# The first two feature tiles of a macaron FFN computed together, k tile by k tile, on one Trainium2 core

## The chip, the core and the metric

The kernel runs on one core of a Trainium2 chip. The metric is the device time of one execution in microseconds (us); the median of the runs of the kernel before is 1067.11 us (three runs, 1066.84 to 1070.1). Engines are named as in the profile: PE is the matrix engine (PEld its weight loads), ACT the scalar engine, DVE the vector engine, POOL the general one, SP the engine that only issues transfers. The names with a q (SPq, ACTq) are the queues on which an engine issues DMAs.

## The reference, cut to what matters

One decoder layer over 512 tokens, model width 1024, FFN width 2816. The change touches only how its first step begins:

```python
def rms_norm(x, g):
    xf = x.astype(jnp.float32)
    y = xf * lax.rsqrt(jnp.mean(xf * xf, axis=-1, keepdims=True) + EPS)
    return (y * g.astype(jnp.float32)).astype(x.dtype)

def swiglu_ffn(x, g, w_gate, w_up, w_down):
    h = rms_norm(x, g)
    return (jax.nn.silu(h @ w_gate) * (h @ w_up)) @ w_down

x = x + 0.5 * swiglu_ffn(x, ffn1_norm, ffn1_w_gate, ffn1_w_up, ffn1_w_down)
...
x = x + merged @ w_out
x = x + 0.5 * swiglu_ffn(x, ffn2_norm, ffn2_w_gate, ffn2_w_up, ffn2_w_down)
```

Between the two FFNs stand two attention branches, which the change leaves as they are.

## The kernel before, in words

**Layout.** x is kept transposed: 8 tiles `x[d]` of 128 model dimensions by 512 tokens. A product of one feature tile (128 of the 2816 features) runs over these 8 tiles, called k tiles here. Everything is float32 in accuracy: each operand is split into a high part that the matrix engine takes directly (`wh`, `xh`) and a rest (`wl`, `xl`), and each product is three matmuls, high by high, high by rest, rest by high. The high part of a weight is a copy on ACT, its rest a subtraction on DVE (`load_w`, L128 to L144, and `split_w`, L115 to L126). For some weights the rest is made otherwise: ACT writes the negated high part and POOL issues a DMA that adds the raw weight (the `adding` branch, L121 to L123). `prep` (L153) makes `xh` on ACT (L161) and `xl` on DVE (L162) from `x[d]` and the norm weight `gains`. The factor of the norm that depends on the token isn't applied to x but to the products.

**The norm's factor.** `square` (L164) squares `x[d]` on ACT, `add_square` (L170) adds the squares on DVE into one tile `ssq`, in a chain, one d after another. `norm_stats` (L177) is a generator with two steps. Its first step is eight tiny matmuls on `ssq` (L181), a small DVE operation (`v`, L183) and a power on POOL (`rstd`, L185). Its second step is four transposes on PE (L189) and a copy on DVE to `rb` (L191). `activate` (L299) needs `rb`: it multiplies gate and up by it, applies silu on ACT, and splits the result into `ah` and `al`.

**The begin block** (L765 to L800) has a hand written order for SP, ACT and DVE: what the code emits first, each of these engines does first. It loads x[0] on ACT's queue and all else on SP's: parts of the first feature tile's gate and up weights, the norm weights `gains`, the x tiles, and then the whole gate and up of the second feature tile (`raws`, L791). In between it emits the splits, `prep`s and `square`s in an order set by d. After the loop come the split of the second tile's gate with the fourth `add_square` inside it, the last four squares, the last four `add_square`s, and the split of the second tile's up. The buffers of `wh` and `wl` are three each and are used in turn, so a split waits until PE has finished with the weights that were made three splits earlier.

**The first FFN** (`ffn`, L202). PE's order is written out by hand throughout. First come the gate and up of feature tile 0 (L696 to L701): for each k tile three matmuls into bank `pg`, three into bank `pu`. Then the list `steps` runs: gate of tile 1 (`run_gate(1)`), up of tile 1, gate and up of tiles 2 and 3, eight steps with `w_down` for these four tiles (`run_down`), and then the steps of the remaining tiles, which take pairs of tiles with fewer products (`pair_steps`). Within gate 1, after k tile 3, PE does the first step of `norm_stats`, after k tile 6 the second (`at_k`, L354). `activate(0)` comes after gate 1, `activate(1)` after up 1. The rests of the weights of tiles 2 and 3 are made by ACT and a POOL DMA (`adding` where f > 1), that of tile 1 by DVE.

**Combinations.** `pair_steps` need x in other combinations (`combine`, L325), made for four k tiles with ten DVE operations and four ACT copies each. They need `rb`; from the first step on, two pieces of the twelve are emitted behind each step. They must stand ready when the first `pair_steps` product starts.

Of the kernel before, what the change touches and what calls it, by code (L numbers as in the profile page):

```python
# [12 lines left out]
F32 = mybir.dt.float32  # L13
F32R = mybir.dt.float32r
# [5 lines left out]
P = 128  # L20
T = 512
NT = T // P
D = 1024
KD = D // P
# [22 lines left out]
PLAIN = 4  # L47
# [8 lines left out]
def tile_hybrid_layer(ctx: ExitStack, tc: tile.TileContext, a: dict):  # L56
    nc = tc.nc
    V, S, G, PE = nc.vector, nc.scalar, nc.gpsimd, nc.tensor

    ctx.enter_context(tc.manual_schedule(engines={mybir.EngineType.PE}))  # L60
    const = ctx.enter_context(tc.tile_pool(name="const", bufs=1))
# [6 lines left out]
    def acc_tile(name):  # L68
        return psum.tile([P, T], F32, tag="acc", bufs=3, name=name)
# [21 lines left out]
    nhalf = const.tile([P, 8], F32, name="nhalf")  # L91
    G.memset(nhalf, -0.5)

    gains = const.tile([P, 3, KD], F32, name="gains")
    xa = const.tile([P, KD, T], F32, name="xa")
    x = [xa[:, d] for d in range(KD)]
    hg = const.tile([P, 4], F32, name="hg")
    bf = const.tile([P, H], F32, name="bf")
# [65 lines left out]
    def square(d, pool=None):  # L164
        sq = (tmp.tile([P, T], F32, tag="ssq", bufs=1, name="ssq") if d == 0 else
              pool.tile([P, T], F32, name=f"sq{d}") if pool else tmp_tile("sq"))
        S.activation(sq, x[d], AF.Square)
        return sq
# [33 lines left out]
    def ffn(n, nxt):  # L202
        wg, wu, wp, wd, wh_ = (a[f"w_{nm}{n}"] for nm in ("gate", "up", "pair", "down", "halves"))
        gi = 0 if n == 1 else 2
        with tc.tile_pool(name=f"ffn{n}", bufs=1) as ap, tc.tile_pool(name=f"halves{n}", bufs=1) as hp:
            act = {}

# [143 lines left out]

            held, pair0, rbs = [], [], []
            stats = norm_stats()
            at_k = (3, 6) if n == 1 else (1, 5)  # L354
            mid = {at_k[0]: lambda: next(stats), at_k[1]: lambda: held.append(next(stats))}

            class Step:

# [8 lines left out]
            def plain(src, f, run, adding=False, ahead=2):  # L367
                raw = {}

                def split():  # L370
                    return [t[:, :f * P].rearrange("p (n m) -> p n m", n=f)
                            for t in split_w(raw["a"][0], f * P, adding)]
                return Step(raw, [("a", f, src)], split, run, "a", ahead)
# [3 lines left out]
            def run_gate(f):  # L377
                def run(w):
                    pg[0] = fm_product(w, "pg", mid if f == 1 else {})
                    if f == 1:  # L380
                        activate(0, *pair0, held[0])
                        rbs.append(held[0])
                return run

            def run_up(f):
                def run(w):

                    pu = fm_product(w, "pu", {}, psum.tile([P, T], F32, tag="s", bufs=2, name="pu1") if f == 1 else None)
                    if f == 0:
                        pair0.extend((pg[0], pu))  # L390
                    else:
                        activate(f, pg[0], pu, rbs[0])
                return run
# [285 lines left out]
            gu_at = cycle(range(4))  # L679
            for lo, hi in GROUPS:  # L680
                for f in range(lo, min(hi, PLAIN)):
                    if f or not first:
                        steps += [plain(wg[f], KD, run_gate(f), f > 1), plain(wu[f], KD, run_up(f), f > 1)]
                for q in range(max(lo, PLAIN) // 2, hi // 2):
                    if ordered[0] is None:
                        ordered[0] = len(steps)
                    steps += pair_steps(q, 2 * q + 2 == hi, lo in HALVED)
                if lo in HALVED:
                    for s in range(2):
                        steps += halved_steps(lo, s)  # L690
                    continue
                ordered[1] = len(steps)
                steps += [plain(wd[d][:, lo:hi], hi - lo, run_down(d, lo, hi), ahead=1 if d == 1 else 2) for d in range(KD)]

            if first:
                pg[0], pu = acc_tile("pg"), acc_tile("pu")  # L696
                for k in range(KD):
                    for ps, w in zip((pg[0], pu), first):
                        PE.matmul(ps, w[k][0], xh[k], start=k == 0, stop=False)
                        PE.matmul(ps, w[k][1], xh[k], start=False, stop=False)  # L700
                        PE.matmul(ps, w[k][0], xl[k], start=False, stop=k == KD - 1)  # L701
                first.clear()
                pair0.extend((pg[0], pu))

            queue = [(i, ld) for i, st in enumerate(steps) for ld in st.loads]
            ws, used = {}, []
# [55 lines left out]
                later.popleft()[0]()  # L762


    first = [[], []]  # L765
    with tc.tile_pool(name="begin", bufs=1) as bp, tc.manual_schedule(
            engines={mybir.EngineType.SP, mybir.EngineType.Activation, mybir.EngineType.DVE}):
        squares = []
        S.dma_start(x[0], a["x"][:, 0, :])
        for d in range(KD):  # L770
            for dst, src, at in zip(first, ("w_gate1", "w_up1"), ({0: (0, 2), 2: (2, 8)}, {1: (0, 4), 4: (4, 8)})):
                if d in at:
                    lo, hi = at[d]
                    w = load_w(a[src][0][:, lo:hi], hi - lo, P, bp.tile([P, 1024], F32, name=f"raw{d}"))
                    dst += [(w[0][:, k], w[1][:, k]) for k in range(hi - lo)]
            if d:
                nc.sync.dma_start(x[d], a["x"][:, d, :])
            else:
                nc.sync.dma_start(gains, a["gains"])
            if d == 6:  # L780
                add_square(0, squares[0])
            if d > 5:
                add_square(d - 5, squares[d - 5])
            prep(d, 0)
            if d > 3:
                squares.append(square(d - 4, bp))
        raws = []
        for nm in ("w_gate1", "w_up1"):
            tag = next(raw_tags)
            raws.append((raw_tile(tag), tag))  # L790
            nc.sync.dma_start(raws[-1][0].rearrange("p (n m) -> p n m", n=KD), a[nm][1])  # L791

        def split_raw(raw, tag, between=None):
            ready.append(([t.rearrange("p (n m) -> p n m", n=KD) for t in split_w(raw, between=between)], tag))

        split_raw(*raws[0], lambda: add_square(3, squares[3]))
        squares += [square(d, bp) for d in range(4, KD)]
        for d in range(4, KD):
            add_square(d, squares[d])
        split_raw(*raws[1])  # L800
# [603 lines left out]
def _fm(w):  # L1404

    k, n = w.shape
    return w.reshape(k // P, P, n // P, P).transpose(2, 1, 0, 3)
# [22 lines left out]
def _layout(x, ffn1_norm, ffn1_w_gate, ffn1_w_up, ffn1_w_down, mix_norm, w_in, b_forget,  # L1430
            fox_q_norm, fox_k_norm, dsa_q_norm, dsa_k_norm, rel_bias,
            w_branch_a, w_branch_b, w_out, ffn2_norm, ffn2_w_gate, ffn2_w_up, ffn2_w_down):
    o = {}
    o["x"] = x.reshape(T, KD, P).transpose(2, 1, 0)
    o["gains"] = np.stack([g.reshape(KD, P).T for g in (ffn1_norm, mix_norm, ffn2_norm)], axis=1)
    o["hgain"] = np.stack([np.concatenate([g, g]) for g in (fox_q_norm, dsa_q_norm, fox_k_norm, dsa_k_norm)], axis=1)
    o["bforget"] = np.broadcast_to(b_forget, (P, H))
    for n, (g, u, dn) in ((1, (ffn1_w_gate, ffn1_w_up, ffn1_w_down)), (2, (ffn2_w_gate, ffn2_w_up, ffn2_w_down))):
        o[f"w_gate{n}"] = _fm(g)[:PLAIN]
        o[f"w_up{n}"] = _fm(u)[:PLAIN]  # L1440

        gu = np.stack([_fm(w)[PLAIN:].reshape(-1, 2, P, 2, HK, P) for w in (g, u)])
        o[f"w_pair{n}"] = gu.transpose(1, 2, 4, 3, 0, 5, 6).reshape(-1, 4, P, 2 * HK * P)
        o[f"w_down{n}"] = _fm(dn)

        dh = _fm(dn)[:, :, PLAIN:].reshape(2, 2, 2, P, -1, GK, 2, P)
        o[f"w_halves{n}"] = dh.transpose(4, 1, 0, 6, 3, 2, 5, 7).reshape(-1, 2, 4, P, 2 * GK, P)
    c = lambda lo, hi: w_in[:, lo:hi]
    o["w_s"] = _tm(np.concatenate([c(2056, 2120), c(2696, 2760), c(2120, 2184), c(1536, 1544), c(2760, 2768)], axis=1))[:, FIRST]
    o["w_fq"] = _tm256(c(0, 512))  # L1450
    o["w_fk"] = _tm256(c(512, 1024))
    o["w_fv"] = _tm256(c(1024, 1536))
    o["w_dq"] = _tm256(c(1544, 2056))
    o["w_iq"] = _fm(c(2184, 2696))
    o["w_ga"] = _fm(c(2768, 3792))
    o["w_gb"] = _fm(c(3792, 4816))
    o["w_ba"] = _fm(w_branch_a)
    o["w_bb"] = _fm(w_branch_b)
    o["w_out"] = _fm(w_out)
    dist = np.maximum(384 + np.arange(P)[:, None] - np.arange(T)[None, :], 0)  # L1460
    o["rel"] = rel_bias[_bucket(dist)].transpose(2, 0, 1)
    return {k: np.ascontiguousarray(v) for k, v in o.items()}
# [19 lines left out]
```

## Time and profile before

| | |
|---|---|
| median of three runs | 1067.11 us |
| the profiled execution, its own time | 1066.31 us |
| its span (first to last instruction) | 1064.6 us |
| granted clock of PE | 1.0 |

The profile is one execution on the chip. Its page gives each engine's busy time and share of the span. The timeline has a row per instruction or run of like instructions: start, duration, engine, line, operation, the tile written and, behind the arrow, the tiles read, shapes, count, and in brackets how long the engine sat idle before it and what released it. The view of waits sums such idle time by the two parties. The DMA view lists each kind of transfer with its size and the median time from issue to landing. The view of windows gives busy time per engine in stretches of the span, and at the end of each row the DMA engines' share and what they moved in GB/s.

### The profile page before, as it was taken

The numbers are of one execution on the slowest core, as the hardware profiler recorded it, in microseconds if no ns is written. First come the engines' busy times: TensorE is split into PE (matmuls) and PEld (weight loads), VectorE is DVE, ScalarE is ACT, GpSimd is POOL, SyncE is SP. The second block draws the span as 40 slices with busy tenths as digits, with TensorE's granted clock in tenths as the row PEclk, the third lists the DMA queues.
The fourth block names the chain that finished last, engine by engine and source line by source line (L and its number), as shares of the span: only waits on it lengthen the run. The fifth ranks groups of instructions, "written<-read, shape, count | busy, mean of one in ns | idle before, by whom it ended". The sixth has DMA issues, their size and how long they took to land.

```text
span 1064.6 us, 19527 instructions
## 1 busy us (share of the span) xinstructions
PE 1051.7 (99%) x7438; PEld 979.8 (92%) x7438; DVE 849.4 (80%) x1400; ACT 672.0 (63%) x1120; POOL 257.2 (24%) x325
## 2 busy tenths in 40 slices
PE   9999999999999999999999999999999999999998
PEld 7889999999999899999877788888889999999998
DVE  6987888887889689977777765853987888887887
ACT  6736765765687675576877665433736765775673
POOL 1100210120121024267777653000100210121111
PEclk9999999999999999999999999999999999999999
DMA  7743754666557358623323321532543665667554
GB/s 241 156 148 111 156 152 139 140 156 181 125 126 179 99 133 201 193 90 110 80 61 120 118 70 50 163 124 81 128 158 100 151 159 147 136 156 183 126 125 129
DMA packets 57917, 143.71 MB, mean 135 GB/s; under 512 B 6616, under 2 KB 15960, under 8 KB 57824
## 3 DMA queue, kind: packets, MB, share of 16 engines
q1 hardware_dynamic: 39888, 110.22, 34.0%
q0 software_dynamic: 17792, 31.99, 17.2%
q8 instruction: 58, 0.95, 0.4%
q10 hardware_dynamic: 144, 0.26, 0.1%
q14 instruction: 35, 0.29, 0.1%
HBM read 104.94 MB, written 3.42 MB: 102 GB/s over the span
## 4 chain that ended last, share of the span: by engine, by line
PE 47%; DVE 3%; POOL 2%; ACT 2%; issue 2%; POOLq 0%; DVEq 0%
PE pB L149 2%; PE pB L151 2%; PE pB L150 2%; PE pA L149 2%; PE pA L151 2%; PE pA L150 2%; PE ps_f L149 2%; PE ps_f L151 2%; PE ps_f L150 2%; PE ps_out L151 1%; PE ps_out L150 1%; PE ps_out L149 1%; PE dB L150 1%; PE dB L149 1%; PE dB L151 1%
## 5 line engine op out<-in xcount | busy, mean ns | idle before, releaser
L118 ACT CAST wh<-s 128x1024 fp32r<-128x1024 f32 (+1 forms) x90 | 86.8, 965 | 66.1 <-PE pC L150 33.2
L125 DVE TENSOR_TENSOR wl<-s,wh 128x1024 fp32r<-128x1024 f32 (+1 forms) x90 | 100.2, 1113 | 27.6 <-ACT wh L118 27.6
L149 PE MATMUL ps_t<-wh,xh 128*128 128x256 f32 (+1 forms) x288 | 81.1, 282 | 0.0
L149 PE MATMUL pB<-tbh,wh 128*128 128x256 f32 x288 | 80.5, 280 | 0.0
L151 PE MATMUL ps_t<-wh,xl 128*128 128x256 f32 (+1 forms) x288 | 80.5, 279 | 0.0
L150 PE MATMUL pB<-tbl,wh 128*128 128x256 f32 x288 | 80.4, 279 | 0.0
L151 PE MATMUL pB<-tbh,wl 128*128 128x256 f32 x288 | 80.3, 279 | 0.0
L150 PE MATMUL ps_t<-wl,xh 128*128 128x256 f32 (+1 forms) x288 | 80.2, 279 | 0.0
L243 POOL DMA_DIRECT2D b<-gu x12 | 10.4, 864 | 222.7 <-DVE rf L443 98.6
L149 PE MATMUL ps_f<-xh,wh 128*128 128x512 f32 x152 | 60.6, 399 | 0.0
L151 PE MATMUL ps_f<-xh,wl 128*128 128x512 f32 x152 | 59.6, 392 | 0.0
L150 PE MATMUL ps_f<-xl,wh 128*128 128x512 f32 x152 | 59.6, 392 | 0.0
L150 PEld LDWEIGHTS ps_t<-wl,xh 128*128 128x128 f32 x288 | 54.3, 189 | 0.4
L149 PEld LDWEIGHTS ps_t<-wh,xh 128*128 128x128 f32 x288 | 54.3, 189 | 0.4
L151 PEld LDWEIGHTS ps_t<-wh,xl 128*128 128x128 f32 x288 | 54.3, 188 | 0.1
L150 PEld LDWEIGHTS pB<-tbl,wh 128*128 128x128 f32 x288 | 54.1, 188 | 0.0
L151 PEld LDWEIGHTS pB<-tbh,wl 128*128 128x128 f32 x288 | 54.1, 188 | 0.0
L149 PEld LDWEIGHTS pB<-tbh,wh 128*128 128x128 f32 x288 | 54.1, 188 | 0.0
L1202 POOL TENSOR_SCALAR p<-p,rs 128x512 f32<-128x512 f32 (+1 forms) x64 | 39.4, 617 | 59.5 <-DVE rs L1201 56.8
L569 POOL DMA_DIRECT2D xa<-e x20 | 23.9, 1241 | 122.3 <-ACT wh L118 102.7
L1200 ACT ACTIVATE p<-p,mn 128x512 f32<-128x512 f32 (+1 forms) x64 | 35.9, 561 | 25.4 <-DVE mn L1198 25.0
L1214 DVE TENSOR_TENSOR pl<-pt,ph 128x512 fp32r<-128x512 f32 (+1 forms) x64 | 31.0, 486 | 18.7 <-ACT ph L1213 18.1
(406 smaller groups left out, 4203.6 us busy)
## 6 DMA issues: line engine op xcount, KB each, us to landing
ra<-in_w_pair_dram SPq DMA_DIRECT2D x15, 512.0 KB, 4.0
rc<-in_w_pair_dram SPq DMA_DIRECT2D x15, 512.0 KB, 4.1
re<-in_w_pair_dram SPq DMA_DIRECT2D x12, 512.0 KB, 3.5
rf<-in_w_pair_dram SPq DMA_DIRECT2D x12, 512.0 KB, 3.6
rb<-in_w_pair_dram SPq DMA_DIRECT2D x12, 512.0 KB, 3.6
xa<-e POOLq DMA_DIRECT2D x22, 256.0 KB, 4.0
rd<-in_w_halves_dram SPq DMA_DIRECT2D x12, 384.0 KB, 4.0
ra<-in_w_halves_dram SPq DMA_DIRECT2D x9, 384.0 KB, 3.2
```

The source lines that it names most:

```text
L118: S.copy(wh[:, :f], raw[:, :f])
L125: V.tensor_sub(wl[:, :f], raw[:, :f], wh[:, :f].bitcast(F32))
L149: PE.matmul(out, lh, rh, start=start, stop=False, **more)
L150: PE.matmul(out, lh, rl, start=False, stop=False, **more)
L151: PE.matmul(out, ll, rh, start=False, stop=stop, **more)
L243: G.dma_start(l, src, accum_op=OP.add)
L569: G.dma_start(xa[:, d:d + 2, HT:], t["e"][part], accum_op=OP.add)
L1200: S.activation(p, p, AF.Exp, bias=mn, scale=-1.0, accum_out=rs)
L1202: G.tensor_scalar(p, p, rs, 1.0, op0=OP.mult, op1=OP.mult)
L1214: V.tensor_sub(pl[:, sl], pt[:, sl], ph[:, sl].bitcast(F32))
```

## The change

The gates and ups of feature tiles 0 and 1 are computed in one block, k tile by k tile: twelve matmuls for each k tile, into four banks (`pg`, `pu`, `pg1`, `pu1`). Their weights come from a new input `w_first`, in which the four 128x128 blocks of one k tile stand side by side, and are loaded in five transfers (2, 6, 8, 8 and 8 blocks). The norm weights stand ahead of x in one input, so that `gains` and x[0] are one transfer. What `raws` loads and splits by DVE is now feature tile 2; only tile 3 is split with a POOL DMA. The first step of `norm_stats` comes after k tile 5 of the block, the second after the first bank's last three matmuls in k tile 7. Both `activate`s follow the block. The steps of the first FFN begin with tile 2. The second FFN is as before.

```diff
-    gains = const.tile([P, 3, KD], F32, name="gains")
-    xa = const.tile([P, KD, T], F32, name="xa")
+    gx = const.tile([P, 3 * KD + KD * T], F32, name="gx")
+    gains = gx[:, :3 * KD].rearrange("p (n k) -> p n k", n=3)
+    xa = gx[:, 3 * KD:].rearrange("p (k t) -> p k t", k=KD)
...
             stats = norm_stats()
-            at_k = (3, 6) if n == 1 else (1, 5)
-            mid = {at_k[0]: lambda: next(stats), at_k[1]: lambda: held.append(next(stats))}
+            mid = {1: lambda: next(stats), 5: lambda: held.append(next(stats))}
...
-                    if f or not first:
-                        steps += [plain(wg[f], KD, run_gate(f), f > 1), plain(wu[f], KD, run_up(f), f > 1)]
+                    if f > 1 or not first:
+                        steps += [plain(w[f - skip], KD, run(f), f > 1) for w, run in ((wg, run_gate), (wu, run_up))]
...
             if first:
-                pg[0], pu = acc_tile("pg"), acc_tile("pu")
+                banks = [acc_tile("pg"), acc_tile("pu")] + [
+                    psum.tile([P, T], F32, tag="s", bufs=2, name=nm) for nm in ("pg1", "pu1")]
                 for k in range(KD):
-                    for ps, w in zip((pg[0], pu), first):
-                        PE.matmul(ps, w[k][0], xh[k], start=k == 0, stop=False)
-                        PE.matmul(ps, w[k][1], xh[k], start=False, stop=False)
-                        PE.matmul(ps, w[k][0], xl[k], start=False, stop=k == KD - 1)
+                    parts = [(i, z) for z in ("hh", "lh", "hl") for i in range(4)]
+                    if k == 0:
+                        parts = [(i, z) for z in ("hh", "lh", "hl") for i in (0, 1)] + [
+                            (i, z) for z in ("hh", "hl", "lh") for i in (2, 3)]
+                    if k == KD - 1:
+                        parts.sort(key=lambda iz: iz[0])
+                    for i, z in parts:
+                        PE.matmul(banks[i], first[4 * k + i]["hl".index(z[0])], (xh, xl)["hl".index(z[1])][k],
+                                  start=k == 0 and z == "hh", stop=k == KD - 1 and z == "hl")
+                        if k == KD - 1 and (i, z) == (0, "hl"):
+                            rbs.append(next(stats))
+                    if k == KD - 3:
+                        next(stats)
                 first.clear()
-                pair0.extend((pg[0], pu))
+                for f in range(2):
+                    activate(f, *banks[2 * f:2 * f + 2], rbs[0])
...
         squares = []
-        S.dma_start(x[0], a["x"][:, 0, :])
+
+        def load_first(lo, hi):
+            raw = bp.tile([P, (hi - lo) * P], F32, name=f"raw{lo}")
+            nc.sync.dma_start(raw, a["w_first"][:, lo * P:hi * P])
+            return [raw, lo, hi]
+
+        def split_first(raw, lo, hi, cuts=()):
+            wh, wl = (wpool.tile([P, 1088], F32R, tag=nm, name=nm) for nm in ("wh", "wl"))
+            edges = (lo, *cuts, hi)
+            for i, j in zip(edges, edges[1:]):
+                c = slice((i - lo) * P, (j - lo) * P)
+                S.copy(wh[:, c], raw[:, c])
+                V.tensor_sub(wl[:, c], raw[:, c], wh[:, c].bitcast(F32))
+            first.extend([t[:, (i - lo) * P:(i - lo + 1) * P] for t in (wh, wl)] for i in range(lo, hi))
+
+        def load_x(d):
+            nc.sync.dma_start(x[d], a["x"][:, 3 * KD + d * T:3 * KD + (d + 1) * T])
+
+        S.dma_start(gx[:, :3 * KD + T], a["x"][:, :3 * KD + T])
+        loads = [load_first(0, 2), load_first(2, 8)]
+        for d in range(1, KD):
+            load_x(d)
+            if d in (2, 4, 6):
+                loads.append(load_first(4 * d, 4 * d + 8))
+        split_first(*loads[0])
         for d in range(KD):
-            for dst, src, at in zip(first, ("w_gate1", "w_up1"), ({0: (0, 2), 2: (2, 8)}, {1: (0, 4), 4: (4, 8)})):
-                if d in at:
-                    lo, hi = at[d]
-                    w = load_w(a[src][0][:, lo:hi], hi - lo, P, bp.tile([P, 1024], F32, name=f"raw{d}"))
-                    dst += [(w[0][:, k], w[1][:, k]) for k in range(hi - lo)]
-            if d:
-                nc.sync.dma_start(x[d], a["x"][:, d, :])
-            else:
-                nc.sync.dma_start(gains, a["gains"])
             if d == 6:
                 add_square(0, squares[0])
             if d > 5:
                 add_square(d - 5, squares[d - 5])
             prep(d, 0)
             if d > 3:
                 squares.append(square(d - 4, bp))
+            if d == 0:
+                split_first(*loads[1], cuts=(4,))
+            if d in (2, 4, 6):
+                split_first(*loads[d // 2 + 1])
         raws = []
...
-            nc.sync.dma_start(raws[-1][0].rearrange("p (n m) -> p n m", n=KD), a[nm][1])
+            nc.sync.dma_start(raws[-1][0].rearrange("p (n m) -> p n m", n=KD), a[nm][0])
```

On the host the new input is `np.stack([_fm(w)[f] for f in (0, 1) for w in (ffn1_w_gate, ffn1_w_up)], axis=2)`, reshaped to 128 rows, and the arrays of the first FFN's plain gates and ups hold only tiles 2 and 3.

More of the change, by code (lines that the diff above doesn't have):

```diff
@@ L204, in ffn @@
         gi = 0 if n == 1 else 2
+        skip = 2 if n == 1 else 0
         with tc.tile_pool(name=f"ffn{n}", bufs=1) as ap, tc.tile_pool(name=f"halves{n}", bufs=1) as hp:
@@ L762, in ffn @@
                 later.popleft()[0]()
-    first = [[], []]
+    first = []
     with tc.tile_pool(name="begin", bufs=1) as bp, tc.manual_schedule(
@@ L1433, in _layout @@
     o = {}
-    o["x"] = x.reshape(T, KD, P).transpose(2, 1, 0)
-    o["gains"] = np.stack([g.reshape(KD, P).T for g in (ffn1_norm, mix_norm, ffn2_norm)], axis=1)
+    gains = np.stack([g.reshape(KD, P).T for g in (ffn1_norm, mix_norm, ffn2_norm)], axis=1)
+    o["x"] = np.concatenate([gains.reshape(P, -1), x.reshape(T, KD, P).transpose(2, 1, 0).reshape(P, -1)], axis=1)
+    o["w_first"] = np.stack([_fm(w)[f] for f in (0, 1) for w in (ffn1_w_gate, ffn1_w_up)], axis=2).reshape(P, -1)
     o["hgain"] = np.stack([np.concatenate([g, g]) for g in (fox_q_norm, dsa_q_norm, fox_k_norm, dsa_k_norm)], axis=1)
@@ L1438, in _layout @@
     for n, (g, u, dn) in ((1, (ffn1_w_gate, ffn1_w_up, ffn1_w_down)), (2, (ffn2_w_gate, ffn2_w_up, ffn2_w_down))):
-        o[f"w_gate{n}"] = _fm(g)[:PLAIN]
-        o[f"w_up{n}"] = _fm(u)[:PLAIN]
+        o[f"w_gate{n}"] = _fm(g)[4 - 2 * n:PLAIN]
+        o[f"w_up{n}"] = _fm(u)[4 - 2 * n:PLAIN]
         gu = np.stack([_fm(w)[PLAIN:].reshape(-1, 2, P, 2, HK, P) for w in (g, u)])
```

## The prediction
> **What bounds the kernel now.** First the page's busy shares, then PE's waits over the first 80 us.
>
> ```profile
> PE 1051.7 (99%) x7438; PEld 979.8 (92%) x7438; DVE 849.4 (80%) x1400; ACT 672.0 (63%) x1120; POOL 257.2 (24%) x325
> ...
> PE pg L699 <- ACT xh L161: 1.1, 2, 0.7
> PE idle L80 <- POOL ones L76: 1.1, 1, 1.1
> PE pg L701 <- DVE xl L162: 0.2, 1, 0.2
> ```
>
> PE is busy 99% of the span, and its order is written by hand. So time lost on PE near the start delays the end by as much, and only that counts. The waits column (total, times, longest) names 1.1 us for `xh` and 0.2 us for `xl`; the timeline shows more.
>
> ```profile
> 5.67 0.79 PE L699 MATMUL pg<-xh,wh 128*128 128x512 f32 x1 [0.41 <-ACT xh L161]
> 6.26 0.63 PE L700 MATMUL pg<-xh,wl 128*128 128x512 f32 x1
> 7.48 0.40 PE L701 MATMUL pu<-xl,wh 128*128 128x512 f32 x1
> 8.57 0.50 PE L699 MATMUL pg<-xh,wh 128*128 128x512 f32 x1 [0.69 <-ACT xh L161]
> 8.91 0.40 PE L700 MATMUL pg<-xh,wl 128*128 128x512 f32 x1
> 11.79 0.40 PE L699 MATMUL pu<-xh,wh 128*128 128x512 f32 x1
> 21.79 0.39 PE L151 MATMUL pg<-xh,wl 128*128 128x512 f32 x1
> 22.02 0.95 PE L181 MATMUL ps_ssq<-ones,ssq 128*128 128x1 f32 x8
> 22.82 0.49 PE L149 MATMUL pg<-xh,wh 128*128 128x512 f32 x1
> ...
> 25.00 0.60 PE L189 MATMUL ps_rb<-ident,rstd 128*128 128x128 f32 x4
> 25.36 0.48 PE L149 MATMUL pg<-xh,wh 128*128 128x512 f32 x1
> 31.61 0.39 PE L149 MATMUL pg<-xh,wh 128*128 128x512 f32 x1
> ```
>
> Starts matter here, since durations overlap. From 11.79 (the 16th matmul of the first block) to 21.79 lie 44 steps: 10.0 us, **0.227 us a matmul** at full pace. The 15 before it took 11.79 - 5.67 = 6.1 us where 15 x 0.227 = 3.4 us would do. The 96 matmuls of tiles 0 and 1 end where gate 2 begins, at 31.61. At full pace they would need 21.8 us, and the statistics take 22.82 - 22.02 = 0.80 us and 25.36 - 25.00 = 0.36 us, 23.0 us in all. From 5.67 to 31.61 is 25.9 us. **No more than 2.9 us (0.27%) is to be won here**, plus what an earlier start gives.
>
> **The change, part by part.** Nothing is removed from PE: the same 96 matmuls and statistics. Each x tile now feeds twelve matmuls (2.7 us) where it fed six, so PE should stop starving once the second x tile is there. But four times 64 KB of weights must arrive and be split for each k tile, and the chain of squares stands behind these splits on ACT and DVE.
>
> *Transfers.* These rows give sizes and two landings.
>
> ```profile
> xa<-in_x_dram SPq DMA_DIRECT2D x7, 256.0 KB, 6.4
> raw<-in_w_up_dram SPq DMA_DIRECT2D x2, 256.0 KB, 4.9
> ra<-in_w_gate_dram SPq DMA_DIRECT2D x1, 512.0 KB, 5.8
> raw<-in_w_gate_dram SPq DMA_DIRECT2D x1, 384.0 KB, 6.2
> xa<-in_x_dram ACTq DMA_DIRECT2D x1, 256.0 KB, 3.8
> raw<-in_w_gate_dram SPq DMA_DIRECT2D x1, 128.0 KB
> gains<-in_gains_dram SPq DMA_DIRECT2D x1, 12.0 KB, 3.6
> ...
> 8.91 0.33 SPq L791 DMA_DIRECT2D ra<-in_w_gate_dram  x1
> ...
> 4.90 0.72 ACT L161 ACTIVATE xh<-xa,gains 128x512 fp32r<-128x512 f32 x1 [0.41 <-DMA gains<-in_gains_dram]
> 7.80 0.72 ACT L161 ACTIVATE xh<-xa,gains 128x512 fp32r<-128x512 f32 x1 [1.67 <-DMA xa<-in_x_dram]
> 8.91 0.83 ACT L138 CAST wh<-raw 128x768 fp32r<-128x768 f32 x1 [0.40 <-DMA raw<-in_w_gate_dram]
> ```
>
> ACT waited at 8.91 for the 384 KB piece, by when 128 + 256 + 12 + 256 + 256 + 384 = 1292 KB had to be in. `ra`, issued at 8.91, landed 5.8 us later, at 14.7, behind three x tiles and a 256 KB weight more before the last three x tiles: 3596 KB. That is (3596 - 1292) / 5.8 = 397 KB/us, and I date every later landing by it. Ahead of the weights of k tiles 4 and 5 there are now 268 + 128 + 384 + 512 + 512 + 512 + 512 = 2828 KB (x[0] with norm weights, two first pieces, x1 and x2, 8 blocks, x3 and x4, 8 blocks): they land at 8.9 + 1536 / 397 = 12.8. x5 comes at 13.4, x6 14.1, the last 8 blocks 15.4, x7 16.0. x1, at 1036 KB, falls between the 908 KB that were in at 7.80 and the 1292 at 8.91: 8.2. Norm weights with x[0] save some 0.2 of the 0.41 us at 4.90; PE starts near 5.4.
>
> *PE.* Its first six matmuls went from 5.67 to 7.71, so k tile 0 ends at 5.4 + 2.04 + 6 x 0.227 = 8.8. `xh` of x1 is done at 8.2 + 0.72 = 8.9. Five k tiles of twelve follow, 13.6 us: **PE stands before the statistics at 22.5**. The weights for k tiles 2 and 3 (landing at 10.2, copied by 11.3, their rest by 12.5) are just in time for 11.6 and 12.6.
>
> *The squares.* Now the order on ACT and DVE, by steps from start to start.
>
> ```profile
> 14.90 0.71 ACT L161 ACTIVATE xh<-xa,gains 128x512 fp32r<-128x512 f32 x1
> 15.52 0.62 ACT L167 ACTIVATE sq<-xa 128x512 f32<-128x512 f32 x1
> 16.04 1.03 ACT L118 CAST wh<-ra 128x1024 fp32r<-128x1024 f32 x1
> 16.98 2.19 ACT L167 ACTIVATE sq<-xa 128x512 f32<-128x512 f32 x4
> 10.65 1.41 DVE L162 SCALAR_TENSOR_TENSOR xl<-xa,gains,xh 128x512 fp32r<-128x512 f32 x2
> 16.57 0.68 DVE L175 TENSOR_TENSOR ssq<-ssq,sq 128x512 f32<-128x512 f32 x1
> 17.18 0.16 DVE L804 TENSOR_SCALAR gq<-hg 128x2 f32<-128x2 f32 x1
> 17.25 1.22 DVE L125 TENSOR_TENSOR wl<-ra,wh 128x1024 fp32r<-128x1024 f32 x1
> 18.38 3.08 DVE L175 TENSOR_TENSOR ssq<-ssq,sq 128x512 f32<-128x512 f32 x4
> ```
>
> On ACT: `xh` 0.62, square 0.52, copy of 1024 columns 0.94. On DVE: `xl` 0.70, one add 0.61, subtraction of 1024 columns 1.13, the four chained adds 3.08. Before, `ssq` was done at 18.38 + 3.08 = 21.46 and PE asked for it at 22.02: no wait. Now, on ACT, the copy for k tiles 4 and 5 starts at 12.9 (landing 12.8; ACT is free of `xh` 4 and square 0 then). Behind it stand `xh` 5, square 1, `xh` 6, square 2: 0.94 + 0.62 + 0.52 + 0.62 + 0.52 = 3.2, so the copy for k tiles 6 and 7 starts at 16.1 and ends at 17.2. From there DVE must do, in its written order, that piece's rest (1.13), an add (0.61), `xl` 7 (0.70), an add (0.61), the rest of gate 2 (1.13) and the four adds (3.08): 7.3 us. Their inputs are there (squares until 21.3, copy of gate 2 until 19.2, its buffer free when k tile 3 ends at 17.1). **`ssq` is done at 24.4 to 24.5.** PE stands from 22.5 to 24.5: a new wait of 2.0 us, since 2048 more columns of weight are split ahead of it.
>
> *The sum.* From 24.5: 0.80 statistics, 15 matmuls 3.4, 0.36 transposes, 9 matmuls 2.0, makes 31.1. A restart after idling costs something: at 8.57 the step to 8.91 was 0.34, 0.11 too long; the three from 5.67 (to 7.02 by the slow steps of 0.59 and 0.43) lost some 0.6. I take 0.3, as 22.82 also follows tiny matmuls and lies near the lower end. Gate 2 starts at **31.4 instead of 31.61: 0.2 us gained**. The rest of PE's order is unchanged.
>
> [...]
>
> *Behind the block.* Gate 2's weights are split by DVE, up 2's too (buffer free at 22.5, needed at 37). Tile 3's POOL DMAs have the place that they had. `rb` is copied near 29.5 rather than 25.64, so combinations start later.
>
> ```profile
> 25.64 0.69 DVE L191 COPY rb<-ps_rb 128x512 f32<-128x512 f32 x1 [2.48 <-PE ps_rb L189]
> 57.33 0.69 DVE L226 TENSOR_TENSOR al<-u,ah 128x512 fp32r<-128x512 f32 x1
> 58.10 0.69 DVE L323 TENSOR_TENSOR tbl<-tb,tbh 128x512 fp32r<-128x512 f32 x1
> 58.36 0.62 PE L657 MATMUL pd<-al,wh 128*128 128x512 f32 x2
> 75.14 0.28 PE L149 MATMUL pA<-b1h,wh 128*128 128x256 f32 x1
> ```
>
> The combinations ended at 58.8 and are first read at 75.14: 16 us of cover, against 4 to 11 us later (4 for `rb`, 11 for two steps of 24 matmuls that no longer carry them). I cost this at nothing. The thin place is `al` of tile 3: done at 58.02, read at 58.36. If DVE is behind there, PE waits; by the row nearest, one combination operation (0.69) to a whole piece, 0.5 to 2 us.
>
> **Rivals.** *PE isn't held at the statistics.* If squares are ready by 22.5, gate 2 starts at 29.1: 2.5 us gained, 1063.8 on the profile's scale. For it: PE itself may come later, and landings may be earlier than dated. Against: DVE's 7.3 us are fixed by order.
>
> *Slower: k tiles 4 and 5's weights land late.* Everything behind their copy on ACT shifts with it, one for one, and past 13.1 the kernel loses. At the pace of an early stretch
>
> ```profile
> 6.00:7.00 1.00, 1.00 (x3) 0.70 (x3) 1.00 (x2) 0.12 (x1) 0.00 (x0) 1.00 0.91 265
> 10.00:11.00 1.00, 1.00 (x5) 0.49 (x3) 1.00 (x2) 1.00 (x3) 0.00 (x0) 1.00 1.05 404
> ```
>
> (265 GB/s, 259 KB/us, instead of 404) they land at 14.8: 1.9 later, 1.7 slower than before, 1068.0. Against it: 4 KB rows and no small pieces in the mix.
>
> *DVE late at `al`:* 1 to 1.5 us slower with the stall above, 1067.5.
>
> *PE's clock drops in the stall:* PE restarts at the pace of 5.67 for some matmuls, 0.6 instead of 0.3 or more, 1066.4 to 1067.5. The windows' clock column is 1.00 in the rows above, and no wait here is 2 us long. [...]
>
> *That the block doesn't run as said* has no way in: PE's order is written out.
>
> **How the numbers follow.** Forecast (the wait eats the gain, within 1 us): 0.58. PE not held: 0.18. Late weights: 0.12. DVE late: 0.08. Clock: 0.04. The sum gives 1066.31 - 0.2 = 1066.1 on the profiled run's scale; the median of the runs lies 0.8 above it, and a later figure will be a median, so I predict **1066.9**. The range takes in the unheld case (1064.6 as a median) and late weights (1068.8, a little more with the clock): 1064.3 to 1069.3. A measurement can tell about 0.3%, 3.2 us. The whole prize is 2.9 us, so faster is 0.04; slower needs weights 3.4 us late or two rivals at once: 0.07; same 0.89.
>
> **What would show it.** Right: no wait of PE from about 9 to 22, then one of some 2 us at L181 released by DVE `ssq`, and gate 2's first matmul within 1 us of 31.6. Wrong: L181 starting by 23 with no wait (then 2.5 us are won), waits for weight copies in k tiles 2 to 5 (transfers slower than dated), or a wait at L657 or at the first `pA`.

## The result, and the profile after

| | before | after |
|---|---|---|
| median | 1066.74 us (6 runs, 1066.52 to 1070.1) | 1072.79 us (6 runs, 1070.87 to 1074.52) |
| profiled execution, span | 1064.6 us | 1070.7 us |
| ratio of the times | | 1.0059, 95% interval 1.0048 to 1.0070 |

The change made the kernel about 6 us slower. The forecast was 1066.9 us, range 1064.3 to 1069.3, with 0.07 for slower by over 0.3%: it was wrong.

The page's row of the engines for the changed kernel:

```profile
PE 1054.2 (98%) x7438; PEld 982.3 (92%) x7438; DVE 851.8 (80%) x1402; ACT 669.4 (63%) x1118; POOL 254.6 (24%) x323
```

PE is busy 98% of a longer span. Its longest waits over the whole execution, from the view of waits (total us, count, longest us); the rows between them belong to other stages and have their like in the kernel before:

```profile
PE ps_t L150 <- ACT wh L139: 1.9, 1, 1.9
...
PE ps_t L151 <- DVE wl L145: 1.3, 1, 1.3
...
PE ps_ssq L182 <- DVE ssq L176: 1.0, 1, 1.0
```

The wait for the squares (L182) is the one forecast. The two longest single waits (1.9 and 1.3 us) are new and lie nowhere near the change: `ps_t` is the first product of the mixing stage, behind the whole first FFN. PE's matmuls come in the same order in both kernels after the first block, so the starts of like matmuls tell where the time went. From the view of one tile (the last numbers are the first and the last start of the group), the first pair of feature tiles after the plain ones, and the projections of the mixing stage, after and then before:

```profile
L150 PE MATMUL pA<-b1h,wh x144: 277/280/288, 75.5 to 1020.4; 128*128 128x256 f32 x144
L150 PE MATMUL ps_f<-xh,wh x152: 387/393/478, 358.0 to 663.0; 128*128 128x512 f32 x152
```

```profile
L149 PE MATMUL ps_f<-xh,wh x152: 387/393/481, 352.6 to 657.1; 128*128 128x512 f32 x152
```

At the first `pA` the changed kernel is 0.4 us behind (75.5 against 75.14, shown ahead of the result), at the first `ps_f` 5.4, at the last 5.9. So the first block lost nothing to speak of, and **nearly all of it was lost between 330 and 358 us**. Both places deserve a look.

**The first block.** The timeline of PE in the changed kernel:

```profile
5.57 0.50 PE L707 MATMUL pg<-xh,wh 128*128 128x512 f32 x1 [0.34 <-ACT xh L162]
...
8.43 0.39 PE L707 MATMUL pg<-xh,wh 128*128 128x512 f32 x1
...
21.80 0.39 PE L707 MATMUL pu<-xl,wh 128*128 128x512 f32 x1
23.17 1.05 PE L182 MATMUL ps_ssq<-ones,ssq 128*128 128x1 f32 x8 [0.98 <-DVE ssq L176]
...
25.55 0.63 PE L707 MATMUL pg<-xh,wl 128*128 128x512 f32 x1
25.98 0.63 PE L707 MATMUL pu<-xh,wl 128*128 128x512 f32 x1
...
28.97 0.40 PE L707 MATMUL pg<-xl,wh 128*128 128x512 f32 x1
29.20 0.60 PE L190 MATMUL ps_rb<-ident,rstd 128*128 128x128 f32 x4
...
31.71 0.39 PE L150 MATMUL pg<-xh,wh 128*128 128x512 f32 x1
```

From 8.43 (the 13th matmul) to 21.80 (the 72nd) lie 59 steps in 13.37 us, 0.227 each: PE runs dense, as hoped. At 22.03 it stops for the squares, 1.1 us. Then, from 25.55, the steps are 0.43 us instead of 0.227, until 28.97. The windows give the clock that was granted to PE, as a share of full speed (third number from the end):

```profile
25.00:26.00 1.00, 1.00 (x6) 0.77 (x5) 0.00 (x0) 0.00 (x0) 0.80 (x1) 0.77 0.94 365
26.00:27.00 1.00, 1.00 (x4) 0.81 (x3) 0.00 (x0) 0.00 (x0) 0.00 (x0) 0.50 1.01 367
27.00:28.00 1.00, 1.00 (x4) 0.81 (x3) 0.00 (x0) 0.00 (x0) 0.00 (x0) 0.50 0.40 154
28.00:29.00 1.00, 1.00 (x4) 0.71 (x4) 0.00 (x0) 0.00 (x0) 0.00 (x0) 0.52 0.00 0
```

The clock was halved. From 25.55 to 28.97 lie 8 steps: 3.42 us where 8 x 0.227 = 1.82 would do, **1.6 us lost** beside the 1.1 us of the wait. Gate 2 starts at 31.71, 0.1 us later than before.

**The seam.** SP's issues for the mixing stage's first three weight chunks (two halves of `w_s`, then `w_iq`), before and then after:

```profile
328.32 0.33 SPq L137 DMA_DIRECT2D ra<-in_w_s_dram  x1
333.42 0.33 SPq L137 DMA_DIRECT2D rb<-in_w_s_dram  x1
337.93 0.33 SPq L137 DMA_DIRECT2D rc<-in_w_iq_dram  x1
```

```profile
322.88 0.33 SPq L138 DMA_DIRECT2D rc<-in_w_iq_dram  x1
332.08 0.33 SPq L138 DMA_DIRECT2D rb<-in_w_s_dram  x1
338.26 0.33 SPq L138 DMA_DIRECT2D ra<-in_w_s_dram  x1
```

The mixing stage takes its buffers in a fixed order, ra, rb, rc. The first FFN gives each load the buffer that has been unused longest (`load`, the choice of `tag`), and in the changed kernel it makes two loads fewer. That turns the assignment round: the last weight that it splits now sits in ra, not in rc. DVE's last subtraction of the stage, before and then after:

```profile
336.96 0.95 DVE L125 TENSOR_TENSOR wl<-rc,wh 128x768 fp32r<-128x768 f32 x1
```

```profile
337.28 0.95 DVE L126 TENSOR_TENSOR wl<-ra,wh 128x768 fp32r<-128x768 f32 x1
```

So the *first* chunk of the mixing stage waits for the buffer that is freed *last*, and goes out ten us later, while rc stands free from 322.9. Timeline of the changed kernel behind it, then the window that follows:

```profile
342.32 0.87 ACT L139 CAST wh<-ra 128x832 fp32r<-128x832 f32 x1
...
343.24 0.36 PE L150 MATMUL ps_t<-wh,xh 128*128 128x208 f32 x1 [1.87 <-ACT wh L139]
344.87 0.36 PE L151 MATMUL ps_t<-wl,xh 128*128 128x208 f32 x1 [1.27 <-DVE wl L145]
```

```profile
346.40:349.80 3.40, 3.40 (x18) 3.40 (x17) 3.37 (x6) 0.80 (x2) 0.00 (x0) 0.50 0.90 314
```

3.1 us of waits, and then again 3.4 us at half clock, worth 1.7 us. The load landed 3.3 to 3.4 us after its issue, at about 341.6; ACT's copy began only at 342.32, since ACT now did two `xh` and two squares ahead of it, which stood behind it before. So some 0.7 us of the first wait is ACT's order, which turns with the buffers. That these cause the loss, and that the buffer causes them, is still only read from one trace; the runs below test it.

### The profile page after: what moved, and what is told of

It is laid out like the page before. It is cut to its first block, busy times and chain, and to the rows that moved or that the text cites. A ratio compares the mean times of both kernels' runs of the same rounds, so it can differ in the third digit from the quotient of the medians.

```text
span 1070.7 us, 19514 instructions
## 1 busy us (share of the span) xinstructions
PE 1054.2 (98%) x7438; PEld 982.3 (92%) x7438; DVE 851.8 (80%) x1402; ACT 669.4 (63%) x1118; POOL 254.6 (24%) x323
## 3 DMA queue, kind: packets, MB, share of 16 engines
HBM read 104.94 MB, written 3.42 MB: 101 GB/s over the span
## 4 chain that ended last, share of the span: by engine, by line
PE 47%; DVE 3%; POOL 2%; ACT 2%; issue 2%; POOLq 0%; DVEq 0%
PE pB L150 2%; PE pB L151 2%; PE pB L152 2%; PE ps_f L150 2%; PE ps_f L151 2%; PE ps_f L152 2%; PE pA L150 2%; PE pA L151 2%; PE pA L152 2%; PE ps_out L150 1%; PE ps_out L151 1%; PE ps_out L152 1%; PE dB L152 1%; PE dB L151 1%; PE dB L150 1%
## 5 line engine op out<-in xcount | busy, mean ns | idle before, releaser
L570 POOL DMA_DIRECT2D gx<-e x20 | 23.9, 1241 | 122.2 <-ACT wh L119 102.0
L1231 ACT ACTIVATE p<-p,mn 128x512 f32<-128x512 f32 (+1 forms) x64 | 35.9, 561 | 24.8 <-DVE mn L1229 24.5
```

The source lines that it names most:

```text
L570: G.dma_start(xa[:, d:d + 2, HT:], t["e"][part], accum_op=OP.add)
L1231: S.activation(p, p, AF.Exp, bias=mn, scale=-1.0, accum_out=rs)
```

## The experiments

Each was timed against the kernel before on the same chip, where before had a median of 1066.26 us (runs 1 to 4) and 1066.24 us (runs 5 to 7).

**1. The kernel before, with the last-freed buffer first.** Is the buffer enough to make the loss, without anything else of the change?

```diff
-    raw_tags = cycle(("ra", "rb", "rc"))     # in the kernel before, for the mixing stage
+    raw_tags = cycle(("rc", "rb", "ra"))
```

> The kernel before, with one change: the mixing stage takes its three raw weight buffers in the order rc, rb, ra instead of ra, rb, rc, so that its first weight chunk goes to rc, the buffer that the first FFN frees last (its load for the third chunk went out at 337.93). Theory A (in the changed kernel 4.9 us are lost at the seam between the first FFN and the mixing stage only because the first chunk's buffer is freed last): the load of the first chunk goes out at 338 instead of 328.3, PE waits some 3 us before the first ps_t matmul, the clock falls to 0.5 for 3.4 us behind it (1.7 us more), and the time is 1071 to 1072 us. Rival B (the seam is late in the changed kernel for another reason, work pushed back or another order on ACT and DVE): within 1 us of before, 1066 to 1068 us.

Measured: 1072.65 us, ratio to before 1.0059 (1.0045 to 1.0072). From its timeline of SP:

```profile
337.28 0.33 SPq L137 DMA_DIRECT2D rc<-in_w_s_dram  x1
```

The longest waits of PE:

```profile
PE ps_t L149 <- ACT wh L138: 2.2, 1, 2.2
...
PE ps_t L150 <- DVE wl L144: 1.2, 1, 1.2
```

And the window behind them:

```profile
345.60:349.00 3.40, 3.40 (x18) 3.40 (x18) 3.37 (x6) 0.98 (x2) 0.00 (x0) 0.50 0.96 311
```

The load goes out as late, the same two waits are there in nearly the same size, the clock falls for as long, and the ratio is the changed kernel's, from a kernel whose first block is untouched. Theory A holds, B falls. The time lies a little above what A gave.

**2. The changed kernel, with a buffer that is free first.**

```diff
-    raw_tags = cycle(("ra", "rb", "rc"))     # in the changed kernel, for the mixing stage
+    raw_tags = cycle(("rc", "rb", "ra"))
```

> The changed kernel, with the mixing stage's buffers in the order rc, rb, ra: the first chunk goes to rc, which is free from 322.9 on. Theory A: no wait before ps_t, no second fall of the clock, 4.9 us less than the changed kernel's 1072.8: 1067.5 to 1068.5 us, 0.5 to 1.5 above before. What is left is the wait of 1 us and the first fall of the clock at 25.4 to 28.8. Rival B: 1072 to 1074 us, with the wait at ps_t still there.

Measured: 1067.1 us, ratio 1.0008 (0.9999 to 1.0017), so 5 us of the 6 are gone. Its timeline:

```profile
323.80 0.33 SPq L138 DMA_DIRECT2D rc<-in_w_s_dram  x1
...
342.40 0.26 PE L150 MATMUL ps_t<-wh,xh 128*128 128x208 f32 x1
342.50 0.28 PE L151 MATMUL ps_t<-wl,xh 128*128 128x208 f32 x1
```

PE enters the mixing stage without a wait. Made by the buffer in one kernel, undone by it in the other: the seam is settled. What is left is the question that the forecast was about, and there the kernel is within a measurement of before, as the forecast had it, though 0.8 us slower where 0.2 us faster was forecast.

**3. The statistics one k tile later.** With the buffers of run 2.

```diff
-                        if k == KD - 1 and (i, z) == (0, "hl"):
-                            rbs.append(next(stats))
-                    if k == KD - 3:
+                    if k == KD - 2:
                         next(stats)
+                rbs.append(next(stats))
```

> As the run with the buffers in the order rc, rb, ra, and in the first block the statistics' first step comes behind k tile 6 instead of 5, the second behind the whole block. Theory C (PE waits 1 us for the squares, and this idle stretch with the tiny matmuls behind it makes the clock fall for 3.4 us, which costs 1.7 us more): PE asks for the squares at 24.7, when they have been done since 23.1, so no wait and no fall of the clock; gate 2 starts at 29.2 to 29.7 instead of 31.71, and the time is 1065 to 1066 us, 2.5 below the run with the buffers alone and 1 to 1.5 below before. Rival D (the wait only moves: the transposes wait for the power on POOL, or silu and the combinations come too late further on): gate 2 at 31 or later, 1067 to 1068.5 us.

Measured: 1065.47 us, ratio 0.9994 (0.9985 to 1.0002), 1.6 us less than run 2. Its timeline, then a window of it:

```profile
24.77 0.95 PE L182 MATMUL ps_ssq<-ones,ssq 128*128 128x1 f32 x8
28.79 0.48 PE L150 MATMUL pg<-xh,wh 128*128 128x512 f32 x1
```

```profile
24.00:27.00 3.00, 3.00 (x19) 2.61 (x18) 0.72 (x2) 0.00 (x0) 0.94 (x1) 1.00 0.84 269
```

No wait at L182, no fall of the clock in the block, and gate 2 starts at 28.79, 2.9 us before the changed kernel's 31.71. Theory C holds in this trace, wait and clock together; run 4 takes them apart. The time gained is less than the 2.5 us that C gave, and 2.8 us ahead of before at gate 2 became 0.8 us at the end, so something gives it back. Runs 5 and 6 look for the part that goes by the first pair; by the traces another 0.9 us goes between the first and the last `ps_f` (350.7 to 656.1, before 352.6 to 657.1), and nothing here says why.

**4. The wait filled with useless matmuls.** With the buffers of run 2; the five products are read by nothing.

```diff
                     if k == KD - 3:
+                        for _ in range(5):
+                            PE.matmul(idle, first[4 * k][0], xh[k], start=True, stop=True)
                         next(stats)
```

> As the run with the buffers in the order rc, rb, ra, and PE does five useless 512 column matmuls (1.13 us) between k tile 5 and the statistics, where it waited 1 us. Theory C: the clock stays at 1.0 from 22 to 32, gate 2 starts at 30.0 to 30.4 instead of 31.71, 1066 to 1067 us: doing more makes it 1.4 us faster than the run with the buffers alone. Rival E (the clock falls whatever PE does there, or at a set time): the clock still shows 0.5 for 3.4 us near 25 to 29, gate 2 at 31.8 or later, 1068 us or more.

Measured: 1066.98 us, ratio 1.0011 (1.0001 to 1.0020): not faster than run 2 with 1067.1, so the gain of 1.4 us that C gave is missed. The trace shows what C says, though:

```profile
22.65 1.30 PE L713 MATMUL idle<-xh,wh 128*128 128x512 f32 x5
...
30.64 0.39 PE L150 MATMUL pg<-xh,wh 128*128 128x512 f32 x1
```

The window in which run 2 had the clock down:

```profile
26.00:29.00 3.00, 3.00 (x16) 2.48 (x16) 0.60 (x3) 0.34 (x1) 1.04 (x1) 1.00 0.72 236
```

Clock 1.0 throughout, and gate 2 at 30.64 (0.2 to 0.6 later than C gave), earlier than the 31.80 of run 2, whose trace has the clock at 0.5 from 24.6 to 28.1. So, in one trace each, the idle wait goes with a fall and the filled one with none. Why the median gains nothing isn't shown. One fall of 3.4 us lowers the granted clock over the span to 0.998 (in run 1's trace the fall is 345.6 to 349.0), and this stands in 6 of 11 executions of run 2, 4 of 12 of run 4, but also 4 of 11 of run 3, without the wait, and 9 of 29 of the kernel before. So falls come elsewhere too, and these counts don't tell the filled wait from chance. Executions at 0.998 are slower than those at 1.0: in the median by 1.7 us in run 2, by 1.5 in run 4 and in the kernel before, by 0.5 in run 3.

**5. The combinations done earlier.** As run 3.

```diff
-                    for _ in range(2):
+                    for _ in range(3 if n == 1 else 2):
                         if next(combos, "end") == "end":
```

> As the run with the statistics one k tile later (buffers rc, rb, ra, which are free in that order here too), and in the first FFN three pieces of the combinations are emitted behind each step instead of two, so that they end with the last up, as in the kernel before. In the run without this, 2.8 us were ahead at gate 2 and 1.8 us behind the first matmuls of the pairs: 0.4 us went at 59.5, 0.7 us near 73.5, where PE waited for a weight whose raw load had to wait for rd, the combinations' buffer. Theory F (the combinations, begun two steps later, are what gives that 1 us back): no wait at 73.5, 2.4 to 2.8 us ahead there, 1064.3 to 1065 us. Rival G (DVE has no room for them earlier, and the rest of tile 3's activation comes late): a wait near 55.5 instead, 1065.5 to 1067 us.

Measured: 1066.11 us, ratio 0.9999 (0.9989 to 1.0010); run 3 had 0.9994 (0.9985 to 1.0002), so no gain, and the two aren't told apart. Its waits of PE in the first 345 us, then tile 3's `al` in its timeline:

```profile
PE pd L658 <- DVE al L228: 1.0, 1, 1.0
```

```profile
56.13 0.69 DVE L228 TENSOR_TENSOR al<-u,ah 128x512 fp32r<-128x512 f32 x1
```

The wait at the first pair is gone, as F has it, and another of 1.0 us stands at `al`: rival G. This was the thin place of the prediction (0.34 us of cover at 58.36), and it gives way as soon as DVE gets more to do ahead of it.

**6. Another buffer for the pairs' third weight.** As run 3; the mixing stage takes rc, ra, rb, in which order they come free here.

```diff
                         combos = None
                         free.add("rd")
+                        used.append("rd")
```

> As the run with the statistics one k tile later, and rd, when the combinations free it, counts as the buffer used last, so that another buffer is given to the pairs' third weight (mixing stage in the order rc, ra, rb, in which the buffers are free here). Theory H (only the choice of rd for that weight makes PE wait at the first pair): no wait near 73.5, 0.4 to 0.7 us less than without, about 1065 us. Rival I (whatever buffer it takes, the load goes out as late, since the others are still in use): the wait stays, 1065.5 us.

Measured: **1064.84 us, ratio 0.9988 (0.9979 to 0.9997)**, the lowest median of all kernels, before included, by 0.1%. DVE's operation on that weight, here and then in run 3:

```profile
68.29 1.22 DVE L441 TENSOR_TENSOR s<-s,rf 128x1024 f32<-128x1024 f32 x1
```

```profile
69.35 1.23 DVE L441 TENSOR_TENSOR s<-s,rd 128x1024 f32<-128x1024 f32 x1 [1.19 <-DMA rd<-in_w_pair_dram]
```

In run 3 DVE sat idle for 1.2 us, waiting for a transfer into rd, which the combinations had just freed; with rf it doesn't wait, and PE has no wait at the first pair. Theory H holds by the traces: PE reaches the first `ps_f` at 350.0 instead of 350.7, though it started gate 2 at 29.12 instead of 28.79. The median is 0.6 us less than run 3's, as H gave, but their intervals overlap, so the time alone doesn't show it.

**7. The norm weights with x alone.** The kernel before, with the joint input.

```diff
-        S.dma_start(x[0], a["x"][:, 0, :])
+        S.dma_start(gx[:, :3 * KD + T], a["x"][:, :3 * KD + T])
...
-                nc.sync.dma_start(x[d], a["x"][:, d, :])
-            else:
-                nc.sync.dma_start(gains, a["gains"])
+                nc.sync.dma_start(x[d], a["x"][:, 3 * KD + d * T:3 * KD + (d + 1) * T])
```

> The kernel before with one part of the change alone: the norm weights stand ahead of x in one input and come with x[0]. Every theory expects the first xh 0.1 to 0.2 us earlier than 4.90, nothing that a measurement can tell: PE still waits for x[1], 1066 to 1067 us, the same as before. [...]

Measured: 1066.29 us, ratio 1.0001 (0.9992 to 1.0010): nothing, as expected. The profiled execution has an odd start:

```profile
5.48 0.72 ACT L162 ACTIVATE xh<-gx 128x512 fp32r<-128x512 f32 x1
...
7.70 0.63 PE L700 MATMUL pu<-xh,wh 128*128 128x512 f32 x1
...
8.13 0.63 PE L701 MATMUL pu<-xh,wl 128*128 128x512 f32 x1
8.56 0.63 PE L702 MATMUL pu<-xl,wh 128*128 128x512 f32 x1
```

The first `xh` comes at 5.48, not before 4.90, because the small first weight piece was late there (ACT waited for it until 5.11); and PE's first matmuls step by 0.43 us, the pace of the half clock. One trace doesn't say whether the late piece belongs to the edit; in the changed kernel, with the same joint input, the first `xh` came at 4.80. The second `xh`, of x[1], starts at 6.93, not after 7.80. The rows of x, which begin 96 B further on here, cost nothing that the time shows (1066.29 us against 1066.24).

## Why the prediction was wrong

**The step that failed** is a sentence at the end of the sum: "The rest of PE's order is unchanged." PE's order is; what PE waits for isn't. The prediction followed the change to the first pair of feature tiles and took the next 250 us as given. It noted the moved loads and even the buffers of `wh` and `wl`, but not that a loop which hands out the least recently used buffer carries two loads fewer to its very end, where another stage has a fixed order. Runs 1 and 2 show this to be worth about 5 us. It could have been read from the code and the SP timeline of before: the three issues at 328, 333 and 338 show that only the third chunk's buffer comes free at the last moment.

**The restart after the wait was mis-sized.** "I take 0.3" stood for 2.0 us: from 23.17 to gate 2 are 8.5 us, and the sum's other terms give 6.6. Of the 2.0, 1.6 are the half clock. The fall of the clock was a rival with a chance of 0.04 and a price of 0.3 or more; it came in this trace, and at both stalls. The rival's upper end, 1067.5 us, was my estimate and stands on no trace; this one shows 1.6 us lost behind the first stall and 1.7 behind the second. I leaned on there being no such wait in the trace of before, and took its slow steps at 5.67 and 6.26 for a restart after idling. They go at the half clock's pace, which the start of the program has (0.43 us from 6.26 to 6.69), though the clock column reads 1.00 there.

**The wait itself was right in kind and too long in size.** Squares were put at 24.4 to 24.5 and PE at 22.5; measured are 23.1 and 22.0, a wait of 1.1 us instead of 2.0. PE came 0.5 us earlier, mainly since its first six matmuls took 1.5 us (5.57 to 7.07), not 2.04. Landings were dated at 397 KB/us from a landing at 8.91; the weights of k tiles 4 and 5, put at 12.8, were copied by ACT without a wait at 11.54 (the timeline of the changed kernel, ACT and DVE):

```profile
11.54 1.04 ACT L792 CAST wh<-raw 128x1024 fp32r<-128x1024 f32 x1
...
20.83 2.28 DVE L176 TENSOR_TENSOR ssq<-ssq,sq 128x512 f32<-128x512 f32 x3
```

The order on ACT and DVE behind that copy took what was worked out (from 11.54 to 23.11 it is 11.6 us; the sum had 11.5).

**The bound was right:** no more than 2.9 us to be won in the block, and run 3 got 2.8 of it against the trace of before (2.4 to 2.6 against those of runs 7 and 1, which have the old block and start gate 2 at 31.19 and 31.43). **Behind the block** the cost wasn't nothing: `al` kept its cover, but the combinations, two steps later, put the pairs' third weight into a buffer that was free too late (in run 3 PE's step from 72.82 to 73.50 at the first pair takes 0.68 us instead of 0.12). The prediction's cover of 16 us counted when combinations are *read*, not when their buffer is *reused*.

The signs that the prediction set for being right came, too: PE without a wait up to 22, then a wait at the statistics released by `ssq`, and gate 2 within 1 us of 31.6. None of them looked behind the first pair, where the time was lost. And by luck, two errors nearly cancelled up to 330 us: a shorter wait and a dearer restart left gate 2 at 31.71, where 31.4 was forecast.

## What to carry to other kernels

When a change adds or drops a load in a stage that hands out buffers in rotation, follow the rotation to the stage's end: which buffer comes free last, and who needs it first. A stage that takes over buffers should ask for the one freed earliest, and SP's issue times show it at a glance. And price a new stall of a microsecond on PE not by its length alone but with what the clock may do behind it (here 1.6 us lost behind a wait of 1.1), together with any tiny matmuls that stand next to it: either move the asker later, or check the clock column, in more than one execution.

## What the runs showed of the hardware

- The clock of PE fell to 0.5 after a stall of only 1.1 us followed by 1 us of tiny matmuls, and not at once: full pace returned at 24.4, and the fall began at about 25.55, lasting 3.4 us. At the seam, after waits of 1.9 and 1.3 us, it was 346.4 to 349.8, again 3.4 us. A stall alone isn't enough: in the same trace PE waits 1.2 us ahead of 521.46 and 1.0 us ahead of 544.31, in the trace of before 1.2 us ahead of 515.74 and of 538.76, and the clock stays at 1.0 behind all four. Nor is the stall at the statistics needed: the profiled executions of runs 5 and 6 have none there, and a granted clock of 0.998 over the span all the same.
- The falls of the changed kernel's profiled execution begin at 25.55, 346.40 and, behind the last matmul, 1070.03: 94 and 306 steps of 3.413 us behind the first. The trace of before has one, at 1065.03, behind its last instruction. Divide these two traces into such steps, each with the offset of its own falls, and count 0.227 us of use for each 512 columns that PE streams. In the four full-clock steps with a fall behind them (two of these at the program's end) PE's use was at most 0.40; in the others behind the first 6.9 us, over 600, it was 0.41 or more. In the changed kernel the step from 22.13 to 25.55 holds the wait and the tiny matmuls whole, and its use is 0.40; the step from 342.99, with the waits of the seam, has 0.38; the step from 520.48, with a wait of 1.2 us, has 0.41, and the clock behind it is 1.0. With another offset the first wait and the tiny matmuls would be divided over two steps; whether that is why the fall doesn't come in each execution wasn't shown. No run varies the use alone, so these are counts from two traces, not a tested limit.
- The half clock's pace, 0.43 us a matmul, also appears at the start of an execution: up to 6.9 in the trace of before, up to 9.4 in run 7, while in the changed kernel the first step from 5.57 is already 0.34 and the next 0.23. How long the start is slow differs between these three executions, and in the trace of before the clock column reads 1.00 throughout it (4 to 7 us).
